# Spare matrix products in the opening of a two-layer block, and its Hyena filters built as sum and difference in one written order

## The chip, the cores and the metric

The kernel is one launch on one core of a Trainium2 chip. The metric is device time in microseconds (us), lower is better. The time before is the median of three runs. A profiled execution gives the trace: the instructions of TensorE (PE for products, PEld for weight loads), VectorE (DVE), ScalarE (ACT) and GpSimd (POOL), and the DMA queue of SyncE (SP). Everything is computed in 32-bit floats or in pairs of them.

## The reference, cut to what matters

The block has two layers on 512 tokens of width 1024, with a context of 256 tokens. Layer 0 mixes by a Fourier half and a Hyena half, layer 1 by attention; each is followed by a convolutional feed-forward stage. The change lies in layer 0, in what computes the modulation, the input projection and the spectrum of the Hyena filter:

```python
sh1, sc1, g1, sh2, sc2, g2 = _adaln(c, w_mod[i], b_mod[i])     # silu(c) @ w_mod + b_mod
hx = _modulate(_rms_norm(x, norm1[i]), sh1, sc1)               # the same for ctx with c_ctx
proj = h @ w_in                                                # 512 Fourier + 3*512 Hyena columns
x0, x1, v = split(_dwconv3(proj[..., 512:], conv_w, conv_b), 3)
# _hyena_filter_spectrum
h = sin(f * (z @ w1 + b1)); h = sin(f * (h @ w2 + b2)); h = sin(f * (h @ w3 + b3))
h = h @ w4                                                     # 64 -> 2 * 512 columns
h_fwd, h_bwd = h[:, :512] * decay, h[:, 512:] * decay
two_sided = concatenate([h_fwd, zeros((1, 512)), h_bwd[:0:-1]])
two_sided = two_sided / sum(abs(two_sided), axis=0)
spectrum = rfft(two_sided, axis=0)
y_h = x0 * (irfft(rfft(v * x1, 2 * L) * spectrum)[:L] + v * x1 * bias)
```

The filter is needed twice, for the 512 tokens and for the 256 of the context.

## The kernel before, in words

**Products in three.** Each big product is split: an operand is a high part (rounded to a 32-bit format that TensorE takes at full rate, written by ScalarE, line 124) and a low part (the rest, written by VectorE, line 129). `mm3` (lines 149 to 151) issues high x high, high x low, low x high. So a weight block (`wload`) costs a DMA into `wr`, a ScalarE pass into `wh` and a VectorE pass into `wl`, in pools of three buffers each. The third product of a group cannot start before `wl` is there.

**The opening** (`mixer`, a block in which the order of PE, DVE, SP and ACT is the written one). The first layer of the filter's small network (line 408) is issued; the squares of x and of the context are summed (lines 265, 272), folded by products with a column of ones (line 278), a chain of small VectorE operations takes the inverse root (lines 158 to 167), and products with the identity spread it over the partitions (line 296). Four chunks of the modulation are products of the condition with 2 MB of weights each (`gemv_pe`: line 216, ScalarE copy line 219, turned by line 224, added to the bias in line 229). Then `both` writes the normed input `hh`, `hl` (lines 306, 307, 311), block by block, and `first` multiplies it with three blocks of `w_in`. In between, layers two and three of the filter network take products (408) and a sine: six VectorE steps (`sine`, lines 382 to 391), then ScalarE's Sin (line 412).

**The filters** (no written order here: a scheduler places the instructions of each engine). For each of six time tiles (4 and 5 for the context, 0 to 3 for x), `filter_mm` takes two products with `w4` (line 421). `filter_pm` multiplies both halves by the decay on VectorE (lines 430, 431), sets row 0 of the backward half to zero in the first tile (433), and lets GpSimd form sum and difference (437), from which ScalarE takes the high parts. ScalarE takes two absolute values (441, 442), GpSimd adds them (443); `filter_lo` writes the low parts. `filter_sum` multiplies with a full block of the constant 256 or 512 (line 459), so that the sum over time stands in all partitions, and takes 128x512 reciprocals on VectorE (461). `filter_spec` multiplies the tiles with a cosine and sine table, `filter_scale` scales by the sum's reciprocal (497, 499; GpSimd adds the bias in 498), `filter_nyquist` makes the row of the highest frequency (475, 477, 478).

**Beside it** run the blocks 3, 4 and 5 of the projection (`proj`, `hconv` with the convolution in lines 371 to 373), and `gemv_dve`: the other 32 column tiles of the modulation are sums of products on VectorE, two passes over 128x1024 and two small additions per tile (lines 241, 242). The list `gl` is worked off wherever the code says so: three tiles beside blocks 4 and 5, 13 beside blocks 8 to 15, eight in the output projection, the rest in the feed-forward stage.

**PSUM.** The tag `mm` has three buffers of 128x1024, taken in turn; `ms` has two of 128x512. A product that wants an `mm` buffer waits until the last reader of the tile three before has finished.

## Time and profile before

| quantity | value |
|---|---|
| median of three runs | 1661.32 us (1657.84, 1661.32, 1666.68) |
| profiled execution, own time | 1657.69 us |
| its span, first to last instruction | 1655.9 us |
| PE busy / PEld busy | 96% / 78% |
| DVE / ACT / POOL busy | 64% / 37% / 8% |
| mean granted TensorE clock | 0.988 |

A row of the timeline reads: start (us from the span's start), duration, engine, line, operation, output and inputs, shape, count, and in brackets how long the engine had been idle before it and what it had waited for. In a table by stretches, each engine has its busy time in the stretch and its instructions; PEclk is the TensorE clock granted there, 1.00 being full speed. A product of 32-bit floats that are not split shows as two records for one instruction.

### The profile page before, as it was taken

To read this page: it belongs to the slowest core of one execution; us is meant where nothing else is said; L and a number is where in the kernel's file an instruction comes from. 1 tells how busy PE (TensorE), PEld (TensorE's weight loads), DVE (VectorE), ACT (ScalarE), POOL (GpSimd) and SP (SyncE) were. 2 spreads that over 40 slices of the span, in tenths; PEclk is the share of its full clock that TensorE was granted. 3 is DMA by queue.
4 is the path that set the end of the run, shared out by engine and by line. 5 is a ranking of instruction groups with operands and counts; after the bars stand their busy time and mean duration, and the time that the engine had idled before them with its cause. 6 is when DMAs were issued, how large, how long until landed. Compare 5 with 4: busy or idle time off the path is not lost.

```text
span 1655.9 us, 20680 instructions
## 1 busy us (share of the span) xinstructions
PE 1588.1 (96%) x8178; PEld 1290.3 (78%) x8178; DVE 1057.4 (64%) x1695; ACT 617.4 (37%) x876; POOL 125.7 (8%) x177
## 2 busy tenths in 40 slices
PE   4989998999999999999998999999999999999999
PEld 2757787888888888888887887666659878878877
DVE  5698969967877354553444576899987544344243
ACT  4432224424222112222122245989864433133131
POOL 0152115000000000000000000222210000000000
PEclk9999999999999999999999999999999999999999
DMA  9325411432444133431430420000014222222222
GB/s 345 132 77 179 173 61 61 170 137 98 156 153 153 64 127 141 142 139 64 140 115 30 146 68 20 13 10 13 1 69 166 85 97 94 90 101 90 89 89 89
DMA packets 54540, 173.34 MB, mean 105 GB/s; under 512 B 6187, under 2 KB 9453, under 8 KB 53421
## 3 DMA queue, kind: packets, MB, share of 16 engines
q1 hardware_dynamic: 54445, 172.03, 29.3%
q8 instruction: 64, 1.05, 0.2%
q14 instruction: 31, 0.25, 0.0%
HBM read 166.24 MB, written 5.77 MB: 104 GB/s over the span
## 4 chain that ended last, share of the span: by engine, by line
PE 77%; DVE 14%; DMA 3%; POOL 2%; ACT 2%; issue 2%; SPq 0%; POOLq 0%; DVEq 0%; ACTq 0%
PE mm L149 23%; PE mm L151 23%; PE mm L150 23%; PE pv L1506 2%; DVE junk L241 2%; DVE wl L129 1%; DVE S L1482 1%; PE s L1452 1%; DMA wr<-wmodT 1%; POOL s L437 1%; DVE wr L1521 1%; PE k L149 1%; PE k L151 1%; PE k L150 1%; DVE mx L1466 0%
## 5 line engine op out<-in xcount | busy, mean ns | idle before, releaser
L149 PE MATMUL mm<-hh,wh 128*128 128x512 f32 (+2 forms) x1360 | 482.5, 358 | 10.6 <-DVE x L373 6.6
L151 PE MATMUL mm<-hh,wl 128*128 128x512 f32 (+2 forms) x1360 | 480.2, 354 | 1.6 <-DVE wl L129 1.6
L150 PE MATMUL mm<-hl,wh 128*128 128x512 f32 (+2 forms) x1360 | 480.3, 354 | 1.4 <-DVE hl L311 1.4
L124 ACT ACTIVATE wh<-wr 128x1024 fp32r<-128x1024 f32 (+2 forms) x192 | 197.6, 1032 | 584.5 <-PE mm L150 554.5
L129 DVE TENSOR_TENSOR wl<-wr,wh 128x1024 fp32r<-128x1024 f32 (+2 forms) x192 | 233.9, 1221 | 254.8 <-ACT wh L124 248.3
L149 PEld LDWEIGHTS mm<-hh,wh 128*128 128x128 f32 x1360 | 257.6, 190 | 58.8 <-issue 14.5
L150 PEld LDWEIGHTS mm<-hl,wh 128*128 128x128 f32 x1360 | 257.9, 190 | 39.5 <-DVE hl L311 2.5
L151 PEld LDWEIGHTS mm<-hh,wl 128*128 128x128 f32 x1360 | 258.0, 190 | 38.4 <-DVE wl L129 1.8
L241 DVE SCALAR_TENSOR_TENSOR junk<-wr,sb 128x1024 bf16<-128x1024 f32 x128 | 157.3, 1229 | 29.8 <-DMA wr<-wmodT 28.8
L151 PE MATMUL mm<-ah,wl 128*128 128x512 f32 (+1 forms) x480 | 172.3, 359 | 0.0
L150 PE MATMUL mm<-al,wh 128*128 128x512 f32 (+1 forms) x480 | 172.1, 359 | 0.0
L149 PE MATMUL mm<-ah,wh 128*128 128x512 f32 (+1 forms) x480 | 172.1, 359 | 0.0
L1048 DVE SCALAR_TENSOR_TENSOR xr<-mm,mod,xr 128x512 f32<-128x512 f32 (+1 forms) x100 | 61.8, 632 | 153.1 <-PE mm L151 152.7
L149 PEld LDWEIGHTS mm<-ah,wh 128*128 128x128 f32 x480 | 90.4, 188 | 14.7 <-issue 0.2
L150 PEld LDWEIGHTS mm<-al,wh 128*128 128x128 f32 x480 | 90.3, 188 | 14.6
L151 PEld LDWEIGHTS mm<-ah,wl 128*128 128x128 f32 x480 | 90.2, 188 | 14.4
L1506 PE MATMUL pv<-S,V 128*128 128x512 f32 x192 | 93.8, 597 | 2.6 <-ACT S L1485 2.6
L1072 ACT ACTIVATE fg<-fg 128x772 f32<-128x772 f32 (+1 forms) x44 | 32.6, 741 | 98.3 <-DVE fg L373 98.3
L1460 ACT ACTIVATE S<-s,rks 128x512 f32<-128x512 f32 x96 | 62.8, 686 | 12.0 <-PE pv L1506 8.0
L1506 PEld LDWEIGHTS pv<-S,V 128*128 128x128 f32 x192 | 34.4, 190 | 34.9 <-issue 29.4
L1478 POOL PARTITION_ALL_REDUCE mx<-mx x16 | 45.2, 2825 | 162.8 <-DVE mx L1475 162.8
L1482 DVE TENSOR_TENSOR S<-S,mx 128x1536 f32<-128x1536 f32 x32 | 55.3, 1749 | 2.3 <-POOL mx L1478 2.3
(330 smaller groups left out, 2266.1 us busy)
## 6 DMA issues: line engine op xcount, KB each, us to landing
wr<-w_up SPq DMA_DIRECT2D x88, 512.0 KB, 3.2
wr<-wmodT SPq DMA_DIRECT2D x80, 512.0 KB, 3.2
wr<-w_dn SPq DMA_DIRECT2D x32, 512.0 KB, 3.2
wm<-wmod0a SPq DMA_DIRECT2D x8, 1024.0 KB, 7.8
wr<-w_in SPq DMA_DIRECT2D x16, 512.0 KB, 3.2
wr<-w_out SPq DMA_DIRECT2D x13, 512.0 KB, 3.2
wr<-w_dn SPq DMA_DIRECT2D x17, 384.0 KB, 3.3
wr<-w_o SPq DMA_DIRECT2D x11, 512.0 KB, 3.2
```

Source lines behind the costliest of these rows:

```text
L124: self.nc.scalar.activation(dst, src, AF.Copy)
L129: (eng or self.nc.vector).tensor_tensor(dst, src, hi.bitcast(F32), op=ALU.subtract)
L149: mmul(out, wh, xh, start=start, stop=False)
L150: mmul(out, wh, xl, start=False, stop=False)
L151: mmul(out, wl, xh, start=False, stop=stop)
L241: nc.vector.scalar_tensor_tensor(junk, raw, 1.0, self.sb[:, j, :], op0=ALU.mult, op1=ALU.mult, accum_out=acc)
L1048: nc.vector.scalar_tensor_tensor(x[m][:, a2:b2], ps[:, a2:b2], mod[:, 8 * sec + m, c : c + 1], x[m][:, a2:b2], op0=ALU.mult, op1=ALU.add)
L1072: nc.scalar.activation(g[:, :n], g[:, :n], AF.Silu)
L1460: nc.scalar.activation(c.S[a][j // 3][:, j % 3, :], c.ps[a, j], AF.Copy, scale=c.r[:, g : g + 1])
L1478: nc.gpsimd.partition_all_reduce(c.m[a][:, 1, :], c.m[a][:, 0, :], P, bass.bass_isa.ReduceOp.max)
L1482: v.tensor_tensor(c.S[a][h], c.S[a][h], mb.to_broadcast([P, 3, T]), op=ALU.subtract)
L1506: nc.tensor.matmul(c.P[a], V[:, j, o : o + 128], c.S[a][j // 3][:, j % 3, :], start=j == 0, stop=j == 5)
```

## The change

Five things are done, all in layer 0, ahead of the block 12 of the projection.

1. **Spare products.** `spare(n)` issues n products of the identity with a constant 128x256 tile into a corner of PSUM that the input projection later overwrites. They stand at seven places of the opening, 8, 5, 3, 3, 1 and 5 of them (25 in all). The first modulation chunk `g0` moves ahead of the spreading of the context's inverse root.
2. **Sum and difference in the weights.** `filter_w4` replaces the two halves of `w4` once by their sum and difference (two additions on GpSimd, a ScalarE copy), so that `filter_mm` yields them directly. `filter_pm` only multiplies by the decay; in the first tile row 0 of both becomes half their sum. |f| + |b| is taken as the larger of |f+b| and |f-b|, on VectorE.
3. **Channel sums as columns.** `filter_sum` multiplies each 128x128 part of the tile with one column of the constant: 4 columns of sums, reciprocals of 128x4, and a later step `spread` (four products with the identity and a ScalarE copy) to lay them out over 128x512.
4. **One written order.** From the copies `Uf` to the end of the spectra the order of PE, DVE, ACT and POOL is the written one. The split of block 3's weights is written ahead of the third sine.
5. **Modulation tiles.** Nine tiles of `gl` are taken ahead of block 12 by this order (before, three), six of them in the loop over the spectra; the output projection takes two (before, eight).

```diff
+    def filter_w4(self):
+        f, b = self.w4[:, 0:512], self.w4[:, 512:1024]
+        t = self.t(self.S2, [P, 512], F32, "s2")
+        self.nc.gpsimd.tensor_tensor(t, f, b, op=ALU.add)
+        self.nc.gpsimd.tensor_tensor(b, f, b, op=ALU.subtract)
+        self.nc.scalar.copy(f, t)
...
     def filter_pm(self, ps, dec, first):
+        s = [self.t(self.S2, [P, 512], F32, "s2") for _ in range(2)]
+        for c in range(2):
+            v.tensor_tensor(s[c], ps[:, 512 * c : 512 * c + 512], dec, op=ALU.mult)
+        if first:
+            r = self.t(self.S2, [P, 512], F32, "s2")
+            v.tensor_tensor(r[0:1, :], s[0][0:1, :], s[1][0:1, :], op=ALU.add)
+            for c in range(2):
+                self.nc.scalar.activation(s[c][0:1, :], r[0:1, :], AF.Copy, scale=0.5)
+        return s
...
+        for c in range(2):
+            self.nc.scalar.activation(s[c], s[c], AF.Abs)
+        v.tensor_tensor(f, s[0], s[1], op=ALU.max)
...
     def filter_sum(self, sums, nhalf):
-            self.nc.tensor.matmul(ps, on, f, start=i == 0, stop=i == len(sums) - 1)
-        self.nc.vector.reciprocal(S, ps)
+        for b in range(4):
+            for i, f in enumerate(sums):
+                self.nc.tensor.matmul(rt[:, b : b + 1], f[:, P * b : P * b + P], self.onesN[nhalf], start=i == 0, stop=i == len(sums) - 1)
+        self.nc.vector.reciprocal(c[:, 0:4], rt[:, 0:4])
+        def spread():
+            R = self.ms()
+            for b in range(4):
+                self.nc.tensor.matmul(R[:, P * b : P * b + P], c[:, b : b + 1].to_broadcast([P, P]), self.ident, start=True, stop=True)
+            self.nc.scalar.copy(S, R)
+            return S
...
+            def spare(n):
+                for _ in range(n):
+                    nc.tensor.matmul(ps3[2][:, 512:768], self.ident, warm, start=True, stop=True)
             pa = layer(0, None, 0)
+            spare(8)
...
             f1(True, 0)
+            spare(5)
             f2(True, 0)
+            spare(3)
             f1(True, 1)
-            f2(True, 1)
             g0 = self.gemv_pe(0, 0, wm[0])
             wm.append(self.gemv_raw(2))
+            f2(True, 1)
             h = layer(0, layer(0, pa, 1), 2)
             g0()
+            spare(3)
...
             pa = layer(1, h, 0)
+            spare(5)
...
+                if d == 4:
+                    self.filter_w4()
+            w3 = self.wload(I["w_in"][3])
             h3 = layer(2, layer(2, pa, 1), 2)
...
+        with self.tc.manual_schedule(engines={ENG.PE, ENG.DVE, ENG.Activation, ENG.Pool}):
...
+            p4 = proj(4, 0, w4)
+            Hs[1] = self.filter_scale(sp1, Sc)
+            nyc = self.filter_nyquist(ac, Sc)
+            self.filter_skip(512.0)
+            gemvs(1)
+            mm_ = {tt: self.filter_mm(h3, tt) for tt in (2, 3)}
+            w5 = self.wload(I["w_in"][5])
+            conv(4, x0[0], p4)
...
+            p5 = proj(5, 0, w5)
+            a3, f3 = self.filter_lo(s3, h3_)
+            wx = self.wload(I["ftab"][0])
+            ax = [a0, a1_, a2_, a3]
+            gemvs(1)
+            spread_x = self.filter_sum([f0, f1_, f2_, f3], 512.0)
+            for ft in range(4):
+                sp = self.filter_spec(ax, wx)
+                if ft == 0:
+                    S = spread_x()
+                    ny = self.filter_nyquist(ax, S)
+                    conv(5, x0[1], p5)
+                wx = self.wload(I["ftab"][ft + 1]) if ft < 3 else None
+                parts = self.filter_scale(sp, S)
...
+                gemvs(2 if ft else 0)
```

Three places show how the order of VectorE moves. The first is at the end of the opening: `ms` is the product of the filter network's third layer, `s_...` its sine, `wl_713` / `wl_685` the low part of block 3's weights, `mm_665` / `mm_727` the first time tile's products. Before:

```order
L311 SCALAR_TENSOR_TENSOR hl_111_349<-s_142_608,mod_4_73,hh_110_348 128x256
L466 TENSOR_SCALAR brow_117<-brow_117 128x512
L382 TENSOR_SCALAR s_143_651<-ms_603,pcol_67 128x384
L384 TENSOR_SCALAR s_144_653<-s_143_651 128x384
L385 TENSOR_SCALAR s_144_653<-s_144_653 128x384
L390 SCALAR_TENSOR_TENSOR s_143_651<-s_144_653,s_143_651 128x384 x3
L391 TENSOR_SCALAR s_143_651<-s_143_651 128x384
L129 TENSOR_TENSOR wl_713<-wr_710,wh_712 128x1024
```

After, at the same place:

```order
L305 SCALAR_TENSOR_TENSOR hl_115_374<-s_144_639,mod_4_73,hh_114_373 128x256
L129 TENSOR_TENSOR wl_685<-wr_682,wh_684 128x1024
L376 TENSOR_SCALAR s_148_688<-ms_634,pcol_67 128x384
L378 TENSOR_SCALAR s_149_690<-s_148_688 128x384
L379 TENSOR_SCALAR s_149_690<-s_149_690 128x384
L384 SCALAR_TENSOR_TENSOR s_148_688<-s_149_690,s_148_688 128x384 x3
L385 TENSOR_SCALAR s_148_688<-s_148_688 128x384
L432 TENSOR_TENSOR s_164_733<-mm_727,s_95_343 128x512
```

The low part of block 3's weights has moved from behind the sine to ahead of it.

The second place is on VectorE around the convolution of block 4 (`x_16`, from `mm_900` / `mm_937`), whose PSUM buffer block 5 takes. `junk` and `mod` are a modulation tile, `brow` the bias row, `apl`, `aml` low parts of a time tile. Before:

```order
L241 SCALAR_TENSOR_TENSOR junk_1073,gacc_1074<-wr_1071,sb_87 128x1024
L466 TENSOR_SCALAR brow_117<-brow_117 128x512
L129 TENSOR_TENSOR apl_890<-s_205_879,aph_881 128x512
L129 TENSOR_TENSOR aml_892<-s_207_883,amh_885 128x512
L242 TENSOR_TENSOR mod_4_73<-gacc_1074,pcol_67 128x1
L241 SCALAR_TENSOR_TENSOR junk_1077,gacc_1078<-wr_1071,sb_87 128x1024
L372 SCALAR_TENSOR_TENSOR x_16_109<-mm_900,pcol_67,x_16_109 128x771
L430 TENSOR_TENSOR s_221_965<-mm_962,s_175_788 128x512
L373 SCALAR_TENSOR_TENSOR x_16_109<-mm_900,pcol_67,x_16_109 128x771
```

After, from the context's Nyquist row (`ms_991`) on:

```order
L491 TENSOR_TENSOR s_221_996<-ms_991,S_870 1x512
L492 TENSOR_TENSOR s_221_996<-s_221_996,brow_117 1x512
L480 TENSOR_SCALAR brow_117<-brow_117 128x512
L235 SCALAR_TENSOR_TENSOR junk_1002,gacc_1003<-wr_1000,sb_87 128x1024
L236 TENSOR_TENSOR mod_4_73<-gacc_1003,pcol_67 128x1
L235 SCALAR_TENSOR_TENSOR junk_1006,gacc_1007<-wr_1000,sb_87 128x1024
L236 TENSOR_TENSOR mod_4_73<-gacc_1007,pcol_67 128x1
L129 TENSOR_TENSOR wl_1019<-wr_1016,wh_1018 128x1024
L366 SCALAR_TENSOR_TENSOR x_16_109<-mm_937,pcol_67,x_16_109 128x771
L367 SCALAR_TENSOR_TENSOR x_16_109<-mm_937,pcol_67,x_16_109 128x771
```

What stands ahead of the convolution is now the Nyquist row, the bias row, a modulation tile and block 5's low part; the time tiles' low parts have gone from there.

The third place is on VectorE at the end of the loop over x's spectra. `wl_1269` / `wl_1383` is the low part of block 12 of `w_in`, the first one multiplied after the spectra; `mm_1146` is the second of the four spectra, `mm_1315` the last. Before:

```order
L497 TENSOR_TENSOR s_266_1171<-mm_1146,S_1089 128x512
L499 TENSOR_TENSOR s_267_1172<-mm_1146,S_1089 128x512
L129 TENSOR_TENSOR wl_1269<-wr_1266,wh_1268 128x1024
L241 SCALAR_TENSOR_TENSOR junk_1391,gacc_1392<-wr_1389,sb_87 128x1024
L242 TENSOR_TENSOR mod_4_73<-gacc_1392,pcol_67 128x1
L241 SCALAR_TENSOR_TENSOR junk_1395,gacc_1396<-wr_1389,sb_87 128x1024
```

After, at the last spectrum:

```order
L511 TENSOR_TENSOR s_300_1340<-mm_1315,S_1171 128x512
L513 TENSOR_TENSOR s_301_1341<-mm_1315,S_1171 128x512
L235 SCALAR_TENSOR_TENSOR junk_1349,gacc_1350<-wr_1347,sb_87 128x1024
L236 TENSOR_TENSOR mod_4_73<-gacc_1350,pcol_67 128x1
L235 SCALAR_TENSOR_TENSOR junk_1353,gacc_1354<-wr_1347,sb_87 128x1024
L236 TENSOR_TENSOR mod_4_73<-gacc_1354,pcol_67 128x1
L235 SCALAR_TENSOR_TENSOR junk_1359,gacc_1360<-wr_1357,sb_87 128x1024
L129 TENSOR_TENSOR wl_1383<-wr_1380,wh_1382 128x1024
```

The split of block 12's weights has moved from right behind the scaling of the second spectrum to behind that of the last one and one and a half modulation tiles.

More of the change, by code (lines that the diff above doesn't have):

```diff
@@ L568, in both @@
                 return a2(d, step)
-            ps3 = [self.mm() for _ in range(3)]
             def first(m, k):
@@ L640, in mixer @@
-        for g in range(3):
-            nc.scalar.copy(Uf[g], ps3[g][:, :TW])
-        with self.tc.issue_after(last.ins), self.tc.issue_after(last_act.ins):
-            tcs = [time_tile(4 + i) for i in range(2)]
-            nc.scalar.copy(Uf[3], proj(3)[:, :TW])
-            nc.sync.dma_start(self.brow, I["hyb"].partition_broadcast(P))
-            self.filter_skip(256.0)
-            tbc = [self.wload(I["ftab"][ft, :, 0:512], 512) for ft in range(2)]
-            self.load_sb()
-            for tt in range(4):
-                dec[tt] = tp()
-                nc.sync.dma_start(dec[tt], I["decay"][tt])
@@ L652, in mixer @@
-        ac = [t_[0] for t_ in tcs]
-        Sc = self.filter_sum([t_[1] for t_ in tcs], 256.0)
+            conv(m, dst, proj(m, ngemv))
+        nc.sync.dma_start(self.brow, I["hyb"].partition_broadcast(P))
+        tbc = [self.wraw(I["ftab"][ft, :, 0:512], 512) for ft in range(2)]
+        for j in range(2):
+            nc.sync.dma_start(self.sb[:, j, :], I["cboth"][j : j + 1, :].partition_broadcast(P))
+        for tt in range(4):
+            dec[tt] = tp()
+            nc.sync.dma_start(dec[tt], I["decay"][tt])
```

133 lines of the change are left out of this document (72 added, 61 removed).

## The prediction

> **What bounds the kernel now.** I read the page first, its list of engines:
>
> ```profile
> PE 1588.1 (96%) x8178; PEld 1290.3 (78%) x8178; DVE 1057.4 (64%) x1695; ACT 617.4 (37%) x876; POOL 125.7 (8%) x177
> ```
>
> PE is busy in 1588.1 of 1655.9 us, so only its idle time can be won, and each new idle time is paid in full unless a later one shrinks. Next I followed PE's timeline from 20 us to block 12, the first product behind the spectra:
>
> ```profile
> 24.71 3.41 PE L216 MATMUL ms<-wm,sT 128*32 128x512 f32 x16 [0.46 <-ACT s L299]
> 29.82 1.92 PE L216 MATMUL ms<-wm,sT 128*32 128x512 f32 x16
> 36.54 0.80 PE L149 MATMUL mm<-hh,wh 128*128 128x512 f32 x1 [2.23 <-ACT hh L307]
> 72.53 3.70 PE L421 MATMUL mm<-w,s 64*128 64x512 f32 x8
> 85.56 1.12 PE L459 MATMUL ms<-s,on 128*128 128x512 f32 x2 [0.66 <-POOL s L443]
> 87.24 1.12 PE L459 MATMUL ms<-s,on 128*128 128x512 f32 x2 [0.55 <-POOL s L443]
> 116.74 0.77 PE L149 MATMUL mm<-hh,wh 128*128 128x512 f32 x1 [6.55 <-DVE x L373]
> 130.42 1.12 PE L459 MATMUL ms<-s,on 128*128 128x512 f32 x2 [1.81 <-POOL s L443]
> 138.87 0.39 PE L149 MATMUL mm<-aph,wh 128*128 128x512 f32 x1
> 144.49 0.40 PE L149 MATMUL mm<-aph,wh 128*128 128x512 f32 x1
> 155.73 0.40 PE L149 MATMUL mm<-hh,wh 128*128 128x512 f32 x1
> ```
>
> From T = 72.53, the end of the first `w_in` products, to block 12 at 155.73 PE idles four times: 0.66, 0.55, 6.55 and 1.81, together 9.57 us. The 6.55 is block 5, which wants block 4's PSUM buffer. One spectrum is 144.49 - 138.87 = 5.62 us. I then asked for stretches around gaps (columns: busy time of PE, PEld, DVE, ACT, POOL, then PEclk, DMA share, GB/s):
>
> ```profile
> 36.00:41.00 5.00, 3.90 (x10) 2.92 (x11) 4.33 (x8) 2.89 (x5) 0.00 (x0) 0.50 1.00 418
> 116.70:118.00 1.30, 1.26 (x3) 1.10 (x4) 1.30 (x3) 0.00 (x0) 0.67 (x1) 0.50 0.00 0
> 118.00:119.50 1.50, 1.50 (x6) 1.31 (x6) 0.99 (x2) 0.00 (x0) 1.50 (x2) 0.50 0.16 19
> 264.00:270.00 6.00, 5.59 (x22) 5.33 (x23) 4.34 (x10) 1.64 (x4) 2.54 (x2) 0.50 0.16 44
> 335.00:350.00 15.00, 15.00 (x66) 12.15 (x65) 14.73 (x28) 4.74 (x6) 0.00 (x0) 1.00 0.50 175
> ```
>
> Behind the 6.55 some 2.8 us run at half clock, 1.4 us lost. The last row is the output projection: PE has no idle there, so the six modulation tiles taken out of it free VectorE but no time.
>
> **The opening: -3.3** (-4.0 to +2.5). In these rows the products begin when `hh` of the normed input is there, and that hangs on VectorE's L306:
>
> ```profile
> 23.06 1.19 PE L296 MATMUL ms<-cst,rq_r 128*128 128x128 f32 x4 [0.93 <-DVE rq_r L167]
> 14.59 2.74 SPq L137 DMA_DIRECT2D wr<-w_in  x3
> wr<-w_in SPq DMA_DIRECT2D x4, 512.0 KB, 13.4
> 31.86 0.59 ACT L219 COPY s<-ms 128x512 f32<-128x512 f32 x1 [1.71 <-PE ms L216]
> 32.35 1.06 ACT L124 ACTIVATE wh<-wr 128x1024 fp32r<-128x1024 f32 x1
> 34.98 2.21 DVE L306 SCALAR_TENSOR_TENSOR s<-x,A,s 128x512 f32<-128x512 f32 x4
> ```
>
> The early `g0`, at full clock, takes 3.41 - 1.92 = 1.5 us off this chain and the spreading of the context's root, the row at 23.06, another 1.2. It cannot come before the first `w_in` block: 14.59 + 13.4 = 28.0, then `wh` twice 2.1, a copy 0.6, a `wl` of 1.2 and small steps of 0.6, so L306 at 32.5, 2.5 us earlier (I take 2.3). Then the 3.90 us of products that ran at clock 0.50 run at 1.00; part of that time waits for `hl` anyhow, so I take 1.0 of at most 2. Together -3.3. The spares themselves are 25 products of 256 columns. The nearest row, 72.53, has four products of 512 columns (two records each) in 3.70, so 0.46 each at full clock, 0.93 at half. PE's idle time there hides them; if they stay at half clock, one group of five stands 2.5 us in the way: the upper bound.
>
> **Block 3's weights ahead of the third sine: +4.4.**
>
> ```profile
> 66.28 0.68 DVE L382 TENSOR_SCALAR s<-ms,pcol 128x384 f32<-128x384 f32 x1 [1.07 <-PE ms L408]
> 69.56 0.36 DVE L391 TENSOR_SCALAR s<-s 128x384 f32<-128x384 f32 x1
> 70.02 0.52 ACT L412 ACTIVATE s<-s 128x384 f32<-128x384 f32 x1 [4.61 <-DVE s L391]
> 70.45 1.04 ACT L124 ACTIVATE wh<-wr 128x1024 fp32r<-128x1024 f32 x1
> 71.52 1.23 DVE L129 TENSOR_TENSOR wl<-wr,wh 128x1024 fp32r<-128x1024 f32 x1 [1.60 <-ACT wh L124]
> ```
>
> Now the sine runs from 66.28 to 69.92 and Sin to 70.54, ready 2 us before PE asks at T. `wh` for block 3 is the fourth in a pool of three: it waits for the last product with the first block's weights, which ends near 70.4, T - 2.1 (the row at 70.45 agrees). After the change VectorE's queue holds `wl` first and the sine behind it: T - 2.1 + 1.04 (`wh`) + 1.15 (`wl`) + 3.64 (sine) + 0.52 (Sin) + 0.15 for the handing over = T + 4.4. PE has nothing else before L421. Bounds: 3.4, if the buffer frees one group (1.05) earlier, and 5.
>
> **Sums, GpSimd, and the 9.57: -11.0.** The sums no longer wait for GpSimd, nor block 5 for the low parts, so the four waits go with 1.4 of cold clock. `filter_w4`'s additions are bounded by GpSimd's nearest row (2.50 for two):
>
> ```profile
> 90.24 3.35 DVE L461 RECIPROCAL S<-ms 128x512 f32<-128x512 f32 x1
> 95.34 2.50 POOL L498 TENSOR_TENSOR s<-s,brow 128x512 f32<-128x512 f32 x2 [8.15 <-DVE s L497]
> 145.90 1.95 DVE L129 TENSOR_TENSOR wl<-wr,wh 128x1024 fp32r<-128x1024 f32 x1
> ```
>
> They lie beside the first `w_in` products, hidden; uncovered, 2.5 + 0.6. The two reciprocals of 3.35 go from VectorE, which counts in the next parts. On PE the sums cost 24 columns, each with a weight load; I price one at a quarter of a 512-column product (0.92), so 5.5, against six products now, 5.5; two spreads of four products of 128 columns at 0.25 and a copy add **+2.3** (0 to 4: a column might cost nearly nothing, or 0.4).
>
> **Block 5 behind block 4: +3.7.** What VectorE now does after the Nyquist row of the context, which needs PE's row behind block 4, stands ahead of block 4's convolution:
>
> ```profile
> 64.78 0.42 DVE L466 TENSOR_SCALAR brow<-brow 128x512 f32<-128x512 f32 x1
> 96.97 0.67 DVE L477 TENSOR_TENSOR s<-ms,S 1x512 f32<-1x512 f32 x1
> 114.05 1.02 DVE L372 SCALAR_TENSOR_TENSOR x<-mm,pcol,x 128x771 f32<-128x771 f32 x1
> 147.76 1.21 DVE L241 SCALAR_TENSOR_TENSOR junk<-wr,sb 128x1024 bf16<-128x1024 f32 x1
> 150.44 0.68 DVE L497 TENSOR_TENSOR s<-mm,S 128x512 f32<-128x512 f32 x1
> ```
>
> Two Nyquist steps 1.2, which overlap a little, bias row 0.4, a modulation tile 150.44 - 147.76 = 2.7, block 5's `wl` 1.15, two convolution steps 1.95: 7.4 us. PE has two time tiles, 3.7, to do meanwhile. What is late next is the same buffer as before: 6.55 becomes 3.7 (2.5 to 6).
>
> **Inside the spectra: +3.9, and +8.8 in two places.** PE is in order, and the third product of a spectrum needs its table's `wl`. For the second spectrum this stands behind the Nyquist steps and block 5's convolution: 1.2 + 1.95 + 1.15 = 4.3, of which PE covers its first two products, 0.46: +3.9. From the end E of the second on, VectorE does: scale (two steps of 0.68, overlapping) 1.2, two tiles 5.4, `wl` 1.15 = E + 7.7; PE wanted it at E + 5.62 + 0.46 = 6.1: +1.7. Then scale 1.2, two tiles 5.4, scale 1.2, one and a half tiles 3.9, block 12's `wl` 1.15: E + 20.6, and PE wants that at E + 6.1 + 1.7 + 5.6 = 13.4: +7.2, together 8.8. The cause is plain: six tiles are 16 us of VectorE in a stretch where PE gives it 5.62 per spectrum. Before, a step was scale, `wl` and one tile, which fits: VectorE's next scaling starts at 150.44, one spectrum after PE's row at 144.49. GpSimd's additions in the scaling remain, and `wl` took 1.95 at 145.90 beside them: up to 0.8 per step more.
>
> The Trainium skill, "SBUF — State Buffer", section "SBUF: two separate sides", says that a VectorE step with two inputs in SBUF and a GpSimd step exclude each other for a whole instruction. By it, as an estimate, each of the additions of 1.25 that are left beside this chain could cost its whole 1.25 where the row shows 0.8; the row decides.
>
> **Cold clock behind the new gaps: +5.6** (0 to 12). Four gaps (4.4, 3.7, 3.9, 7.2) are of the kind that cost 1.4 behind the 6.55. A shorter one cost more:
>
> ```profile
> 262.16 0.30 PE L149 MATMUL ms<-wh,s 128*128 128x128 f32 x1 [2.65 <-DVE e L870]
> ```
>
> Behind it 264 to 270 ran at 0.50, 3 us lost, hence 12 as the bound; one that keeps its clock costs nothing.
>
> The Trainium skill, "TensorE: Matmul & The Clock Gate", section "What's actually happening", puts the gate at half clock after an idle window of about 3.4 us and at full after as long a busy one. By it each of the four loses 1.7, which gives 6.8 for this term; the 2.65 above, which cooled without such a window, says that the phase decides.
>
> **Behind the spectra: 0.** VectorE enters the next blocks with 3.5 tiles (9.4 us) of backlog, but has room there:
>
> ```profile
> 157.00:231.00 74.00, 70.16 (x403) 61.12 (x402) 55.88 (x97) 15.77 (x17) 9.11 (x7) 1.00 0.45 157
> ```
>
> 18 of its 74 us are idle; without that cover, up to +9.4.
>
> **The sum:** -3.3 + 4.4 - 11.0 + 2.3 + 3.7 + 3.9 + 8.8 + 5.6 = +14.4. The profiled execution took 1657.69, which gives 1672.1; the median of the runs shown, 1661.32, is 3.6 above it and gives 1675.7. I say 1674.
>
> **The rivals.**
> *Covered.* The gaps are there but small: the clock stays warm (-5.6), the wait at the sine is the lower 3.4, and about 5 us of the spectra's delay is won back because GpSimd and ScalarE hold VectorE less than before. That is +2 to +6, 1660 to 1667, around 1664. For it speaks that the backlog is VectorE's, idle a third of the time; against it that every one of these waits is in a written order that nothing reorders.
> *Heavier.* Spares at half clock (+2.5 in place of -3.3: 5.8 more), 3 us of cold clock behind each of four gaps (6.4 more), VectorE slowed by 0.8 in each of three steps (2.4 more): +29 if all of it comes, +23 to +28 for most of it, 1681 to 1686. The row at 264 speaks for it, the one at 118 against.
> *The written order hides its splits* (faster). If VectorE's step in the loop comes to no more than PE's 5.62, and block 3's `wh` finds its buffer early enough, none of the new waits arises: -3.3 - 11.0 + 2.3 = -12.0, 1645.7 by the profiled execution, 1649 by the median. It decides at the step of scale, two tiles and `wl`: 7.7 by the rows. It must lose 2.1 us, four halves of a tile's 1.2 each becoming 0.7. The steps here are all 1.2, so little speaks for it.
> *Not what it says*: if the opening's products begin no earlier, the sum is +17.7, still inside the forecast.
>
> **How the numbers follow.** A measurement of this kernel can tell about 0.5%, 8.3 us, from no change: 1653.0 to 1669.6. The forecast, 1670 to 1680, has 0.65, heavier 0.10, covered 0.17, faster 0.08. So slower by over 0.5% has 0.75, within it 0.17, faster 0.08. The range 1662 to 1686 holds the forecast, the heavier case and half of the covered one, some 0.83.
>
> **What would show it.** In the changed profile: L421's first product behind a wait of about 4.4 on ScalarE's Sin; block 5 behind about 3.7 on the convolution; the third products of the second spectrum, the last spectrum and block 12 behind 3.9, 1.7 and 7 on a `wl`; PEclk 0.50 for some 3 us behind each but the 1.7; no wait on GpSimd at the sums; the first `w_in` product 2 us earlier with PEclk 1.00. The prediction is wrong if L421 follows without a wait, or if VectorE reaches block 12's `wl` before PE ends the last spectrum.

## The result, and the profile after

The changed kernel takes 1679.63 us (median of four, 1678.02 to 1681.26) where the kernel before takes 1659.58 (four, 1657.08 to 1666.68): the ratio is 1.0122, with a 95% interval of 1.0098 to 1.0147. It is slower by 20 us; 1674 was forecast, with a range of 1662 to 1686. The profiled execution spans 1676.5 us (before, 1655.9). The engines' line and PE's timeline of the changed kernel, at the places of the rows shown of before:

```profile
PE 1609.4 (96%) x8280; PEld 1309.7 (78%) x8280; DVE 1050.0 (63%) x1702; ACT 621.8 (37%) x883; POOL 101.0 (6%) x161
```

```profile
21.62 1.92 PE L210 MATMUL ms<-wm,sT 128*32 128x512 f32 x16 [0.68 <-ACT s L293]
34.53 0.50 PE L149 MATMUL mm<-hh,wh 128*128 128x512 f32 x1
74.24 7.19 PE L415 MATMUL mm<-w,s 64*128 64x512 f32 x8 [4.39 <-ACT s L406]
95.64 3.74 PE L415 MATMUL mm<-w,s 64*128 64x512 f32 x4
116.91 1.99 PE L415 MATMUL mm<-w,s 64*128 64x512 f32 x8
124.90 0.77 PE L149 MATMUL mm<-hh,wh 128*128 128x512 f32 x1 [6.00 <-DVE x L367]
149.99 0.50 PE L149 MATMUL mm<-aph,wh 128*128 128x512 f32 x1 [0.67 <-ACT wh L124]
153.99 0.80 PE L151 MATMUL mm<-aph,wl 128*128 128x512 f32 x1 [3.27 <-DVE wl L129]
169.42 0.50 PE L151 MATMUL mm<-aph,wl 128*128 128x512 f32 x1 [2.50 <-DVE wl L129]
180.78 0.59 PE L149 MATMUL mm<-hh,wh 128*128 128x512 f32 x1 [4.40 <-ACT wh L124]
183.60 0.80 PE L151 MATMUL mm<-hh,wl 128*128 128x512 f32 x1 [1.81 <-DVE wl L129]
291.97 0.44 PE L149 MATMUL ms<-wh,s 128*128 128x128 f32 x1 [2.66 <-DVE e L944]
```

The waits on GpSimd are gone, and the new ones stand where the written order puts a step that PE wants behind other work: 4.39 at the time tiles, 6.00 at block 5, 3.27 and 2.50 inside the second and the last spectrum, 4.40 and 1.81 at block 12. Block 12 starts at 180.78 where it started at 155.73, 25 us later. The last row has its twin in the prediction (262.16 before): by then the kernel is 29.8 us behind, and 9.2 us come back further on.

The stretches of the changed kernel around its waits (columns as in the prediction: busy time of PE, PEld, DVE, ACT, POOL, then PEclk, DMA share, GB/s):

```profile
74.20:81.30 7.10, 7.06 (x8) 2.50 (x8) 1.97 (x3) 1.15 (x3) 0.00 (x0) 0.50 0.23 87
81.30:85.00 3.70, 3.70 (x12) 3.07 (x12) 2.83 (x5) 3.32 (x7) 0.00 (x0) 0.50 0.00 0
124.80:129.50 4.70, 4.60 (x14) 3.97 (x15) 4.00 (x7) 3.62 (x6) 0.00 (x0) 0.50 0.24 92
135.60:139.20 3.60, 3.60 (x36) 3.60 (x34) 0.91 (x3) 0.00 (x0) 0.00 (x0) 1.00 0.60 230
141.00:143.50 2.50, 2.50 (x7) 1.91 (x7) 0.00 (x0) 0.00 (x0) 0.00 (x0) 0.50 0.00 0
12.00:292.00 280.00, 244.56 (x1233) 192.30 (x1231) 203.36 (x368) 84.76 (x124) 35.48 (x41) 0.91 0.40 145
```

and the whole stretch up to the same point before the change:

```profile
12.00:262.20 250.20, 222.01 (x1145) 174.34 (x1145) 196.83 (x326) 79.91 (x118) 60.25 (x57) 0.97 0.41 150
```

PE's idle time grew from 28.2 to 35.4, by 7.2 us only, since less of it lies in the opening; the waits from the filters to block 12 alone grew from 9.6 to 23.0. The clock granted fell from 0.97 to 0.91. Length times missing clock is 7.5 us before and 25.2 after, 17.7 more: the larger part of the loss is half clock, not waiting. These figures come from a clock with two decimals and count idle time too; each is good to about 1.4 us. The 7.5 is also low, for in the profile of before PEclk reads 1.00 in the opening's stretch below, although the modulation chunk at 24.71 takes 3.41 there and 1.92 at full clock. What the opening lost by that is in its own term.

```profile
22.00:32.00 10.00, 7.63 (x45) 2.92 (x44) 5.38 (x13) 3.05 (x6) 0.00 (x0) 1.00 0.91 350
```

### The profile page after: what moved, and what is told of

It is laid out like the page before. It is cut to its first block, busy times and chain, and to the rows that moved or that the text cites. A ratio compares the mean times of both kernels' runs of the same rounds, so it can differ in the third digit from the quotient of the medians.

```text
span 1676.5 us, 20878 instructions
## 1 busy us (share of the span) xinstructions
PE 1609.4 (96%) x8280; PEld 1309.7 (78%) x8280; DVE 1050.0 (63%) x1702; ACT 621.8 (37%) x883; POOL 101.0 (6%) x161
## 4 chain that ended last, share of the span: by engine, by line
PE 78%; DVE 15%; issue 2%; ACT 2%; DMA 2%; POOL 1%; POOLq 0%; SPq 0%; DVEq 0%; ACTq 0%
PE mm L149 23%; PE mm L151 22%; PE mm L150 22%; DVE junk L235 2%; PE pv L1580 2%; DVE wl L129 2%; DVE S L1556 1%; PE s L1526 1%; DVE wr L1595 1%; PE mm L415 1%; DVE hl L305 1%; PE k L149 1%; PE k L150 1%; PE k L151 1%; DMA wr<-w_in 1%
## 5 line engine op out<-in xcount | busy, mean ns | idle before, releaser
L149 PE MATMUL mm<-hh,wh 128*128 128x512 f32 (+2 forms) x1360 | 483.1, 358 | 12.3 <-DVE x L367 6.0
```

The source lines that it names most:

```text
L149: mmul(out, wh, xh, start=start, stop=False)
```

## The experiments

**Block 3's split back behind the sine.**

```diff
-            w3 = self.wload(I["w_in"][3])
             h3 = layer(2, layer(2, pa, 1), 2)
+            w3 = self.wload(I["w_in"][3])
```

Expected: 

> The changed kernel with one step moved back: block 3's weights are split behind the third sine, as in the kernel before. Theory 'queue' (each new wait is VectorE's written order, and what it costs is its own length and the half clock behind it): the wait of 4.4 us at L415 goes, the 10.6 us of half clock behind it go too (5.4 us lost there), and nothing else is late instead, so about 9.8 us less: 1670 us. Rival 'carried on' (VectorE has too much work in this stretch, and time won at one place is lost at the next): the waits ahead of block 5 and in the spectra grow by most of it, under 4 us less: 1676 us or more. Rival 'clock' (the half clock behind L415 has another cause, for instance the low rate of these products): 4.4 us less, 1675 us, with PEclk 0.50 from L415 on as before.

Measured: 1669.53 us (ratio to before 1.0065, interval 1.0043 to 1.0086). PE's timeline, and the stretch from these products to the end of block 3:

```profile
69.25 3.70 PE L415 MATMUL mm<-w,s 64*128 64x512 f32 x8
```

```profile
69.20:81.50 12.30, 12.30 (x57) 8.90 (x56) 7.79 (x13) 7.82 (x15) 0.00 (x0) 1.00 0.13 45
```

The wait is gone and PEclk is 1.00 all through. 10.1 us were won against 9.8 expected: "queue", and both rivals fall. One wait of 4.4 us had cost ten.

**Block 4's convolution first.**

```diff
+            w5 = self.wload(I["w_in"][5])
+            conv(4, x0[0], p4)
             nyc = self.filter_nyquist(ac, Sc)
             self.filter_skip(512.0)
-            gemvs(1)
             mm_ = {tt: self.filter_mm(h3, tt) for tt in (2, 3)}
-            w5 = self.wload(I["w_in"][5])
-            conv(4, x0[0], p4)
...
-            gemvs(1)
+            gemvs(2)
             spread_x = self.filter_sum([f0, f1_, f2_, f3], 512.0)
```

Expected: 

> The changed kernel with the order around block 4 rewritten: block 5's weights and block 4's convolution stand ahead of the Nyquist row and the bias row, and the modulation tile is taken one step later, with the next one. Theory 'queue': block 5's wait of 6.0 us falls to what the convolution itself takes behind block 4 (1.0 on ScalarE and 2.0 on VectorE, against 0.9 and 2.0 of PE work), so under 1 us, and 2.3 us of half clock in block 5 go: 7 to 8 us less, 1672 us. Rival 'carried on': the third time tile is late for the sums or its table for the first spectrum, and 3 us or less are won: 1676.5 us or more.

Measured: 1676.35 us (1.0103, 1.0083 to 1.0123), 3.3 less than the changed kernel. Its timeline at block 5 and at x's sums, and the clock there:

```profile
120.61 0.47 PE L149 MATMUL mm<-hh,wh 128*128 128x512 f32 x1 [0.44 <-DVE x L367]
129.11 5.05 PE L464 MATMUL ms<-on,s 128*128 128x1 f32 x32
```

```profile
131.50:134.00 2.50, 2.50 (x14) 2.50 (x15) 2.43 (x6) 0.00 (x0) 0.00 (x0) 0.54 0.57 200
134.00:138.00 4.00, 4.00 (x10) 3.15 (x11) 2.79 (x8) 0.00 (x0) 0.00 (x0) 0.50 0.52 159
```

The wait fell from 6.00 to 0.44 and block 5's cold start went, as "queue" had it, and at the transforms (286.71 against 291.97) 5.3 us of it are left. The sums as columns took 4.9 us where they had taken 3.5, half of that at half clock. So the place is right and the gain smaller than the 7 to 8 expected: some went to the next cold stretch, and only 3.3 of the 5.3 reach the end.

**The loop over the spectra.**

```diff
                 sp = self.filter_spec(ax, wx)
+                wx = self.wload(I["ftab"][ft + 1]) if ft < 3 else None
                 if ft == 0:
...
                     conv(5, x0[1], p5)
-                wx = self.wload(I["ftab"][ft + 1]) if ft < 3 else None
...
-                gemvs(2 if ft else 0)
+                gemvs(1 if ft else 0)
```

Expected: 

> The changed kernel with the loop over the spectra rewritten: each next table is split ahead of the Nyquist steps, the convolution and the scaling, and one modulation tile is taken in each of the last three steps where two were (three tiles go back to the output projection). Theory 'queue': the waits of 3.3 and 2.5 us inside the spectra go with the half clock behind them (5.1 and 4.5 us by the lengths of these two spectra), and of the 4.4 and 1.8 us ahead of block 12 at most 1 is left: 14 to 17 us less, 1664 us, of which the three tiles may take back 1 in the output projection. Rival 'buffers' (the raw weights share three buffers with the tiles, so the load comes late whatever VectorE's order is): the waits ahead of block 12 stay at 3 us or more and some 8 us are won: 1671 us.

Measured: 1670.03 us (1.0063, 1.0041 to 1.0085), 9.6 less. Its timeline from the second spectrum to block 12 and behind:

```profile
154.36 0.50 PE L151 MATMUL mm<-aph,wl 128*128 128x512 f32 x1 [0.58 <-DVE wl L129]
165.46 0.50 PE L149 MATMUL mm<-hh,wh 128*128 128x512 f32 x1
166.72 0.50 PE L151 MATMUL mm<-hh,wl 128*128 128x512 f32 x1 [0.53 <-DVE wl L129]
193.51 0.98 PE L769 MATMUL mm<-cst,tm 128*128 128x128 f32 x6 [1.69 <-DVE tm L762]
212.60 0.98 PE L769 MATMUL mm<-cst,tm 128*128 128x128 f32 x6 [1.15 <-ACT tm L365]
```

12.0 us of waits became 1.1, the one at block 12's load included. So "buffers" falls in the form in which it was put, that the load comes late whatever VectorE's order is; as the run also takes three modulation tiles fewer, which frees buffers earlier, it does not tell the order's part from theirs. Block 12 starts at 165.46, 15.3 earlier; at the transforms 13.5 are left. "Queue" fits, though less reached the end than expected: two small waits came up behind block 12, and the stages behind were 1.7 us longer than in the changed kernel's profile.

**Channel sums with a full block again.**

```diff
-        for b in range(4):
-            for i, f in enumerate(sums):
-                self.nc.tensor.matmul(rt[:, b : b + 1], f[:, P * b : P * b + P], self.onesN[nhalf], ...
-        c = self.t(self.sm, [P, 24], F32, "fsum")
...
+        for i, f in enumerate(sums):
+            self.nc.tensor.matmul(rt, self.onesN[nhalf], f, start=i == 0, stop=i == len(sums) - 1)
+        S = self.t(self.pf, [P, 512], F32, "S")
+        self.nc.vector.reciprocal(S, rt)
+        return lambda: S
```

Expected: 

> The changed kernel with the channel sums formed as before: a full block of the constant against each time tile, a reciprocal of 128x512 on VectorE, no columns and no spreading. Theory 'thin products cool the clock' (PE counts as busy in the columns, but the clock falls to half behind them): PEclk stays 1.00 behind the sums, the second time tile takes 1.9 where it took 3.7, the context's first spectrum is 0.8 shorter and x's first 1.6 shorter; with 3 to 4 us of columns and spreading that go, 7 to 8 us less: 1672 us. Rival 'another cause for the half clock' (the gaps ahead): PEclk is 0.50 at these places as before, and only the columns' own 3 us go: 1676.5 us. If the two reciprocals of 3.35 us delay the spectra, a new wait on VectorE of up to 3 us shows ahead of x's second spectrum.

Measured: 1680.79 us (1.0128, 1.0107 to 1.015), no less than the changed kernel. Its stretches behind the two sums, and its timeline there and further on:

```profile
97.10:99.00 1.90, 1.90 (x6) 0.66 (x5) 1.80 (x1) 0.00 (x0) 0.00 (x0) 1.00 0.00 0
137.70:143.70 6.00, 6.00 (x27) 4.56 (x26) 3.36 (x1) 0.03 (x1) 0.00 (x0) 1.00 0.08 33
```

```profile
97.09 1.98 PE L415 MATMUL mm<-w,s 64*128 64x512 f32 x4
150.31 0.79 PE L151 MATMUL mm<-aph,wl 128*128 128x512 f32 x1 [4.14 <-DVE wl L129]
178.28 0.79 PE L149 MATMUL mm<-hh,wh 128*128 128x512 f32 x1 [6.02 <-ACT wh L124]
289.87 0.44 PE L149 MATMUL ms<-wh,s 128*128 128x128 f32 x1 [2.65 <-DVE e L934]
```

The clock stays at 1.00 and the second time tile takes 1.98 where it took 3.74: the theory's mechanism is there. The gain is smaller than the 7 to 8 expected. The second spectrum starts 4.5 us earlier (145.54 against 149.99); the waits in the loop grew a little (4.14 for 3.27, 6.02 for 4.40), so that block 12 starts 2.5 us earlier, and 2.1 are left at the transforms (289.87 against 291.97). That the time is no shorter has its reason behind them: from there to the end this kernel takes 5.9 us longer (1390.4 against 1384.5), 4.1 of it in the last feed-forward stage. It lacks the two small tiles of the column sums, and the experiment with unused tiles below bears on that stage. By the whole time alone the theory could not be judged.

**All four repairs.** The three edits above and full-block sums; besides, each table is split two steps ahead, block 4's weights right behind the context's sums, blocks 12 and 8 inside the written order, and of the modulation tiles three fewer than in the kernel with the loop repaired are taken up to the inverse transforms.

```diff
+            wx = [self.wload(I["ftab"][0])]
...
+            wx.append(self.wload(I["ftab"][1]))
...
+                wx.append(self.wload(I["ftab"][ft + 2] if ft < 2 else I["w_in"][12 if ft == 2 else 8]))
                 parts = self.filter_scale(sp, S)
```

Expected: 

> The changed kernel with all four repairs at once: block 3's split behind the third sine, block 4's convolution ahead of the Nyquist row, channel sums with a full block, and a loop over the spectra in which each weight block is split two steps ahead, block 12 and block 8 included, with one modulation tile a step. Theory 'queue': no wait over 1 us is left between the first w_in products and block 12, which then starts near 140 us of the span where the kernel before started at 155.7; with the opening's 2.7 and the stage behind as before this gives 1640 to 1648 us. Rival 'carried on' (VectorE's work is the limit of the whole stretch up to the inverse transforms, so waits come up in the blocks 12 to 15 and 8 to 10 instead): 1655 us or more.

Measured: 1645.34 us, faster than before (0.9937, 0.9918 to 0.9955). Its largest wait up to block 12, block 12, and the loop's stretch:

```profile
106.67 0.47 PE L149 MATMUL mm<-hh,wh 128*128 128x512 f32 x1 [1.20 <-DVE x L367]
142.99 0.40 PE L149 MATMUL mm<-hh,wh 128*128 128x512 f32 x1
```

```profile
124.30:142.90 18.60, 18.60 (x81) 14.25 (x80) 18.00 (x29) 3.19 (x3) 3.86 (x3) 1.00 0.57 197
```

PE has no idle time in the loop and VectorE 0.6 us: "queue", though one wait of 1.20 is over the 1 that it allowed. The three single repairs won 10.1, 3.3 and 9.6 us, 23.0 together, and all at once 34.3. So the opening, sum and difference and a written order as such can stay in a kernel that is faster than before. What the further shifts of this run are worth by themselves, and sum and difference without the rest, no run shows.

**The same with columns.** The sums of the change put back into the repaired kernel. Expected: 

> The repaired kernel (all four repairs) with the channel sums as columns and spreading again, as in the changed kernel, and nothing else altered. Theory 'thin products cool the clock': behind both sums PEclk is 0.50 for some 3 to 5 us; with the columns' and spreads' own time, 3 to 4 us, block 12 starts 6 to 8 us later than in the repaired kernel (143.0 us of the span), and since VectorE has room there nothing is given back: 1652 us. Rival 'VectorE': the reciprocals of 3.35 us that columns save on VectorE are worth as much there, block 12 starts within 3 us of 143, and the time is 1646 to 1648.

Measured: 1645.69 us (0.9923, 0.9899 to 0.9947). Its block 12, its transforms, and the clock behind the first sums:

```profile
151.25 0.40 PE L149 MATMUL mm<-hh,wh 128*128 128x512 f32 x1
259.24 0.45 PE L149 MATMUL ms<-wh,s 128*128 128x128 f32 x1 [2.66 <-DVE e L944]
```

```profile
88.00:92.00 4.00, 4.00 (x12) 2.18 (x10) 3.65 (x6) 1.15 (x2) 0.00 (x0) 0.50 0.65 238
```

Block 12 starts 8.3 us later, of which 1.6 is the opening's: the theory is right about the place. Yet the time is the same. Against the changed kernel, which has the same sums, this run changes the order and the places of the modulation tiles alone, and is 33.9 us faster: the loss lay there. As for the columns, the profiles put the difference behind the transforms, where this kernel takes 1384.9 us and the other 1391.9. Here too only the kernel with columns has the two small tiles. The last run below, full blocks with the tiles added, is the fairer partner: it reaches the transforms 8.7 us earlier (250.57 against 259.24) and takes 1639.33 us, 6.4 less. With the tiles in both, columns cost about what the theory says; the two times are from different rounds.

**The opening alone, and the change without its spare products.** The first is the kernel before with `spare` and the early `g0`; in the second the body of `spare` does nothing. (The products stand at six places, as the diff has them, not at seven.)

Expected: 

> The kernel before with the opening's part of the change alone: the 25 spare products at their seven places and the first modulation chunk ahead of the spreading of the context's root; filters and their order as before. Theory 'opening' (the prediction's term): the first w_in product starts 2 us earlier with PEclk 1.00, the products end at 69.9 where they ended at 72.5, and the gain stays: 2.7 us less, 1657.8 us beside the 1660.5 of before. Rival 'taken back' (the third sine or block 3's split is then late): the products end earlier but block 12 does not start earlier, 1660 us.

Expected: 

> The changed kernel without the 25 spare products, the first modulation chunk still ahead of the context's spreading. Theory 'opening': PEclk falls to 0.50 in the opening, the first chunk takes 3.4 where it took 1.9, and the first w_in products end about 2 us later: 1681.6 us. Rival 'the early chunk does it': the products start as early without the spares, no more than 0.5 us is lost.

Measured: 1652.74 us (0.9974, 0.9952 to 0.9997) and 1691.96 us (1.0216, 1.0193 to 1.0238). The opening alone, its first `w_in` product, the end of these products and block 12:

```profile
35.10 0.50 PE L149 MATMUL mm<-hh,wh 128*128 128x512 f32 x1
70.37 3.70 PE L421 MATMUL mm<-w,s 64*128 64x512 f32 x8
153.55 0.40 PE L149 MATMUL mm<-hh,wh 128*128 128x512 f32 x1
```

and the changed kernel without the spares:

```profile
22.58 3.64 PE L210 MATMUL ms<-wm,sT 128*32 128x512 f32 x16 [0.68 <-ACT s L293]
38.84 0.80 PE L149 MATMUL mm<-hh,wh 128*128 128x512 f32 x1 [0.67 <-ACT hh L301]
80.07 2.92 PE L415 MATMUL mm<-w,s 64*128 64x512 f32 x3 [4.39 <-ACT s L406]
```

The opening alone brings block 12 forward by 2.2 us, as expected, and nothing takes it back. The time fell by 5.2 (from a median of 1657.91 in that round), more than that: in the profile the stretch from the transforms on is 5.8 us shorter than before (1387.9 against 1393.7), without any change there. The clock records (a trace's list of its stretches at half clock; the loss is half of PE's busy time in them) put 3.1 of it down to less half clock, and 2.6 are less waiting. How much of that a second profile would show is not known. Without the spares the modulation chunk takes 3.64 again and the first products end 5.8 us later (80.07 - 4.39 = 75.68, against 69.85), later than in the kernel before. So the gain is the spares', 5.8 where 2 was expected; the early chunk without them is no gain. The kernel is 12.3 us slower, and its profiled execution, the slowest of four, 18.5 us: 7.1 are there at the transforms and 11.4 come behind them. Of these, by the clock records, 7.0 are more half clock and 3.7 more waiting; why there is more, so far from the spares, no run shows.

**The kernel before once more, and two unused tiles.** The first is a second profile of the same kernel. The second adds the two small tiles that the column sums allocate; what is added to the computation is only that they are cleared. In its trace PE, VectorE, ScalarE and GpSimd execute the same instructions in the same order as before, and VectorE the two that clear:

```diff
         self.nc.vector.reciprocal(S, ps)
+        c = self.t(self.sm, [P, 24], F32, "fsum")
+        self.nc.vector.memset(c[:, 0:4], 0.0)
```

Expected: 

> The kernel before, unchanged, profiled once more. The last feed-forward stage, from its wait of 1.6 us on to the end, took 377.9 us in the profile of before and 372.6 in that of the changed kernel, with the same products at PEclk 1.00 in both. Theory 'execution': its length differs between executions of one kernel, so here it may be anything from 372 to 378. Rival 'kernel': it is 377 to 378 again, and the changed kernel gains 5 us there.

Expected, in the kernel before: 

> The kernel before with one thing added that computes nothing used: the two small tiles of 128x24 that the changed kernel's column sums allocate, each cleared once at the start (two small VectorE steps in its idle time). They move what is allocated behind them by 192 bytes in each partition; the order of all engines is else the same. Theory 'placement' (the stages behind the spectra run faster in the kernels that have these tiles because of where their operands lie): the last feed-forward stage takes 372 to 376 us where the two profiles of before have 377.9, the stretch from the transforms on is 4 to 9 us shorter than 1394, and the time falls to 1651 to 1656 beside 1660. Rival 'not placement' (the code ahead or chance): the last stage takes 377 to 378 us and the time is that of before.

Expected, in the repaired kernel: 

> The repaired kernel with full-block sums and the same two unused tiles added. Theory 'placement': its last feed-forward stage falls from 376.2 to 372 to 375 us and it is 4 to 9 us faster than 1645.3, some 1637 to 1641. Rival 'not placement': 1645 us, as without the tiles.

Measured, from the wait of 1.6 us ahead of the last feed-forward stage to the end of the span: 377.9 us in the second profile of before (1656.7 - 1278.77), 375.4 with the tiles (1655.3 - 1279.90), 372.6 in the repaired kernel with the tiles (1633.5 - 1260.90) against 376.2 without. The rows from which that is counted, the first of the second profile of before, the others of before and of the repaired kernel with the tiles:

```profile
1278.77 0.39 PE L151 MATMUL mm<-hh,wl 128*128 128x256 f32 x1 [1.63 <-DVE wl L129]
```

```profile
1279.90 0.38 PE L151 MATMUL mm<-hh,wl 128*128 128x256 f32 x1 [1.63 <-DVE wl L129]
```

```profile
1260.90 0.39 PE L151 MATMUL mm<-hh,wl 128*128 128x256 f32 x1 [1.63 <-DVE wl L129]
```

and the transforms of the repaired kernel with the tiles, and the first microseconds of the stage in the first profile of before:

```profile
250.57 0.30 PE L149 MATMUL ms<-wh,s 128*128 128x128 f32 x1 [2.65 <-DVE e L936]
```

```profile
1282.20:1287.20 5.00, 4.22 (x30) 4.02 (x28) 1.94 (x9) 0.46 (x2) 0.00 (x0) 0.83 0.37 127
```

The times are 1658.48 (one run), 1656.62 (0.9979, 0.9956 to 1.0003) and 1639.33 us (0.9877, 0.9851 to 0.9903). The two profiles of before agree within 0.1 us, against "execution". In 13 profiles the stage takes 376.2 to 377.9 in the five without the tiles and 372.6 to 375.8 in the eight with them. PEclk is not 1.00 in all of them, as was assumed: in the last row it is 0.83. In seven of the 13 the clock records have half clock at the start of the stage, which costs 1.7 us in six and 3.4 in one. Without it the stage takes 376.1 to 376.6 in the five and 372.3 to 373.7 in the eight, and PE's idle time there is 4.8 to 5.0 in all, so what sets the two groups apart lies in the pace of the products.

The time does not follow as plainly. In the kernel before the whole stretch from the transforms on is 1394.8 us with the tiles, where 4 to 9 less than 1394 was expected: half clock cost 15.7 us between the transforms and the last stage (9.9 and 12.1 in the two profiles without them), which took the gain back. The time's interval includes no change. In the repaired kernel the time is 6 us less, of which 3.6 are in the last stage; the two kernels ran in different rounds. By the code the tiles move what lies behind them by 192 bytes in each partition. That this is what PE feels is likely, not shown: the two steps that clear them are also two VectorE instructions more.

## Why the prediction was right or wrong

Right in direction and range, and in where PE waits and behind what; too low by two thirds in the half clock, and inside its range only with 9 us that came back from a place that it had put at 0. Term by term, up to the inverse transforms:

| term | forecast | measured |
|---|---|---|
| opening | -3.3 | -2.7 |
| wait at the third sine | +4.4 | +4.39 |
| the four old waits and their cold clock | -11.0 | gone |
| spreading of the sums | +2.3 | +2.5 (1.7 and 0.8) |
| block 5 | +3.7 | +6.00 |
| second spectrum | +3.9 | +3.9 (0.67 and 3.27) |
| last spectrum and block 12 | +8.8 | +8.7 (2.50, 4.40, 1.81) |
| cold clock | +5.6 | +17.7 (25.2 less 7.5, by the stretches) |
| behind the transforms | 0 | -9.2 |

The measured terms overlap a little (the 1.4 of cold clock in the third is in the 7.5 as well), so their sum is near the 20.6 us of the two spans and not exact.

*The waits.* At two of four places (the third sine, the second spectrum) their length came out within 0.1 us by adding VectorE's steps in the written order. The last place is right as a sum but not in kind, and that its parts, 2.50 and 6.21 where 1.7 and 7.2 stood, add up to within 0.1 is luck. The last spectrum waited 2.50, since a tile's first step ahead of it took 1.94 beside GpSimd's addition (the 0.8 that the prediction kept as a bound). Block 12, which was to wait for its low part alone, waits mostly for its high part: the load could only start when the second modulation tile behind the third spectrum freed one of the three raw buffers, at 176.4. VectorE, SyncE's queue and ScalarE in the changed kernel:

```profile
162.07 1.94 DVE L235 SCALAR_TENSOR_TENSOR junk<-wr,sb 128x1024 bf16<-128x1024 f32 x1
175.21 1.22 DVE L235 SCALAR_TENSOR_TENSOR junk<-wr,sb 128x1024 bf16<-128x1024 f32 x1
```

```profile
176.47 0.33 SPq L137 DMA_DIRECT2D wr<-w_in  x1
```

```profile
179.67 1.06 ACT L124 ACTIVATE wh<-wr 128x1024 fp32r<-128x1024 f32 x1 [18.34 <-DMA wr<-w_in]
```

*Block 5.* The step that failed is "PE has two time tiles, 3.7, to do meanwhile". Tiles 2 and 3 lie in different halves of the partitions and take 1.99 together (the row at 116.91). The 3.70 came from the row at 72.53, tiles 4 and 5, in the same half. That is 1.7 of the 2.3 us that were missing; VectorE's queue, priced at 7.4, took 7.7 (117.02 to 124.75). A price has to come from the same tiles, not from the same line.

*The cold clock* is the term that was mis-sized: 1.4 behind each gap, from one row. Behind L415 it was 5.4, since PEclk stayed 0.50 for 10.8 us, through seven in which PE worked on products with 64 rows (74.20 to 81.30). Behind block 5's 6.00 it was 2.3, behind the two waits in the spectra 1.8 and 2.0 by the lengths of these spectra. And 4.2 more, by the lengths of the products behind them, stand where the prediction saw nothing: behind the columns, with no gap at all (141.00 to 143.50; the second time tile at 95.64). That the columns cost no more than the products they replace was right (1.9 and 3.5 us); that the next products run at half clock was missed. The kernel with full-block sums has PEclk 1.00 at both places. These five parts make 15.7 of the 25.2; the rest lies in the idle time itself, behind block 12 and ahead of the transforms. In the clock records of the traces half clock comes in pieces of 3.41 us, or two to four of them on end. Up to the transforms the kernel before has four (its records begin at 28 us). The changed kernel has fourteen: four at L415, two each at block 5 and block 12, one at each of the two waits in the spectra, three at the columns, one further on. So a wait's price went by the number of pieces, each worth up to 1.7, and not by the wait's length; the prediction's 5.6 is little more than three of them.

*Behind the transforms* the prediction had 0, and 9.2 us came back: 5.3 in the last feed-forward stage (377.85 to 372.55), 1.7 of them a piece of half clock that the kernel before has at its start, and the other 3.6 what the experiment with unused tiles finds; 1.5 in the output projection (from its first product to the first one behind it 77.0 before, 75.5 after), where the kernel before has another piece; the rest is spread over attention and the first feed-forward stage. So the 1674 came out near by luck as well: the loss ahead was 30, not 14, and a third of it came back from places that no part of the change addresses. Without that the time would have been near 1689, above the range.

*The rivals.* "Heavier" has the size of the cold clock, but not through the spares, which did their work; ahead of the transforms the loss is as large as its whole sum, 29. "Hides its splits" was the other side: it named VectorE's step against PE's 5.62 as the point from which it decides, and the repaired kernel, with one tile a step instead of two, is past that point: no wait in its loop, VectorE busy for 18.0 of 18.6 us. "Covered" did not come: what came back did so far behind the filters, by a way that it did not name.

The Trainium skill, "TensorE: Matmul & The Clock Gate", section "What's actually happening", has the gate go by how busy PE was in a window of about 3.4 us. By it, as an estimate, the term would have been 6.8 against the 5.6 taken; both are far under the 17.7. The pieces of 3.41 us agree with such a window, and so does block 5, with half clock for about 4.7 us of its work; behind L415 it does not, unless products that use half the rows do not count as busy, which the page does not say.

## What to carry to other kernels

In a written order, add up, for each product that PE wants, what stands ahead of its weight split on each engine: that sum gave two of four places to 0.1 us, and a mended order with full-block sums turned a loss of 20 us into a gain of 13. Price a wait with the half clock behind it, which here cost three quarters as much as the waits themselves, and more than the wait where the next products were thin (5.4 behind 4.4). Judge a repair where its stage ends as well as by the whole time: full-block sums were 2.1 us ahead at the transforms and yet no faster, since the stages behind took 5.9 us longer.

## What the runs showed of the hardware that was not expected

- 25 products without use, in time in which PE was idle, are worth 5.8 us in the opening: with them the modulation chunk takes 1.92, without 3.64.
- The clock falls to 0.50 behind 8 or 16 instructions that multiply into a single column, though PE is shown busy all the while (135.60 to 139.20: 3.60 of 3.60). It does so at both sums in all six profiles that have columns, and at neither in the three that have full blocks in the written order.
- Once at 0.50 behind a wait, it stayed there through 7.1 us of 64-row products without a gap (74.20 to 81.30).
- Two unused tiles of 96 bytes in each partition, with the two steps that clear them, shorten a stage that begins over a thousand microseconds later by 2.5 us in one kernel and 3.6 in another, at the same products and the same half clock. Why, no run shows.
- The fastest kernel of the study, the repaired one with these tiles, takes 1639.33 us: 1.2% less than the kernel before and 2.4% less than the changed one.
